# Conditioning sections and broadcasts of a decoder block moved between TensorE and the other engines

## The chip, the cores and the metric

The kernel runs on one core of a Trainium2 chip. The core has five engines with instruction streams of their own: TensorE (matmuls; PE in the profile), VectorE (DVE), ScalarE (ACT), GpSimd (POOL) and SyncE (SP), whose queue here starts nearly all loads from memory. Each engine executes its instructions in order and waits on semaphores for the others. The metric is the time of one execution on the device in microseconds (us); lower is better.

## What is computed

A decoder block for T = 256 tokens of D = 1024 channels, in float32. A conditioning vector `c` gives six rows that shift, scale and gate; then come a projection to 8192 columns, a convolution branch and a gated recurrence, and a mixture of 32 experts of which each token uses 4.

```python
mod = c_act @ w_ada[l] + b_ada[l]          # c_act = silu(c); six rows of 1024
sh1, sc1, ga1, sh2, sc2, ga2 = split(mod, 6)
h = rmsnorm(x, g_mix) * (1.0 + sc1) + sh1
p = h @ w_in[l]                             # 1024 x 8192
y_conv = conformer_conv(p[conv a], p[conv b], ...)   # 31 taps, layernorm, silu, projection
y_hg   = hgrn2(p[q], p[f], p[i], p[g], ...)          # recurrence, norm, gate, projection
merged = sigmoid(p[gc]) * y_conv + sigmoid(p[gh]) * y_hg
x  = x + ga1 * (merged @ w_out)
h2 = rmsnorm(x, g_ffn) * (1.0 + sc2) + sh2
x  = x + ga2 * moe(h2, w_router, b_router, w1, b1, w2, b2)   # top 4 of 32 experts, SwiGLU
out = rmsnorm(x, g_final)
```

## The kernel before

**Loads.** All weights come in tiles of 1 MB (128 partitions of 8 KB) into a ring of 22 slots (`big`, `NSLOT`). `load()` (L123) issues the next tile of a fixed order on SP's queue; the table `LOADS` says how many loads are issued each time a slot is given back by `free()`, and `fetch()` returns a tile. A load whose slot is still in use waits on SP's queue, and so do all behind it. At most eight loads are under way, since each takes one of eight semaphores.

**Start.** ScalarE squares x, TensorE adds the squares up (`ssp`), ScalarE copies the result (`sss`), TensorE gives the total to all partitions (`ss`), and ScalarE and VectorE make `rs` = 1/rms (L225). The first third of the conditioning (shift and scale 1) comes in eight tiles of `w_ada` ("ada0"), each through `mod_first` (TensorE, then a copy `mod0s` on ScalarE) and `h_tile`, which makes one eighth of `h`. This part stands in a block whose order on TensorE, ScalarE and VectorE is given by hand; behind it a scheduler of the framework puts each engine's instructions in order.

**Products.** The 32 blocks of `w_in`, n = 0 to 31 (128 x 8 x 256), are split in two halves each into a high and a low part (`split_half`): ScalarE casts (L371), GpSimd or VectorE subtracts (L373), by the tables `SPLIT_DVE` and `SPLIT_HALF`. "Unit n" is block n. `block_product` then runs 48 matmuls (L387). Blocks 0 to 3 are done during the start. What comes out of a block goes on: sigmoids (L695), 31 conv taps for each of 8 channel tiles (L438, VectorE, 240 steps), the recurrence (`hgrn_half`), and behind all taps a layer norm, whose sums TensorE makes (`mup`, `mu`) and which stands on TensorE ahead of block 25. Behind block 31 come the projections `ho`, `co` and `wo`, four units each, split like the blocks.

**Conditioning, later sections.** `mod_section(j)` makes one of four other rows: j = 1 gives `sh2`, 2 gives `g2`, 3 gives `ga2`, 0 gives `ga1`. Each has four chunks of `w_ada`, (j,0) to (j,3), 128 x 2 x 1024. One step is taken behind each block n in `MOD_AT`: 5, 7, 8, 11 for j = 1; 12 to 15 for j = 2; 18, 22, 25, 26 for j = 3; 27, 28, 30, 31 for j = 0. A chunk is 8 matmuls of 32 rows (L327), in which the column of `c_act` is the stationary operand; the results of the four column groups are copied (`mods`) and picked out by further matmuls (`mt`, `bb`) or, for `ga1`, by four broadcasts of GpSimd (L348, L349). `b_ada` is one loaded tile, added by matmuls for j = 0 and 3. In `hgrn_out` four more broadcasts of GpSimd (L605) give the norm `orr` to all partitions (`ors`).

**Experts.** For each expert, `first_layer` (L981) uses 8 tiles of w1, `turn` (L998, L1001) transposes the result, and `second_layer` (L1014) uses 4 tiles of w2. The rows of w1's tiles are 8 KB for each partition; w2's tile is read as "(k p) d -> p k d", two pieces of 4 KB for each partition.

Of the kernel before, what the change touches and what calls it, by code (L numbers as in the profile page):

```python
# [1402 lines left out]
```

## Time and profile before

| what | value |
|---|---|
| median of 3 runs | 1365.07 us (1362.7 to 1365.19) |
| profiled execution | 1363.14 us, its span 1361.4 us |
| granted TensorE clock, mean | 0.974 |
| busy: TensorE / VectorE / ScalarE / GpSimd | 1239.0 / 493.4 / 236.1 / 151.2 us |
| read from memory | 477.63 MB |
| products' first block behind the start (n=4) | from 59.96 us |
| first expert's products | from 399.34 us |

The profile is of one execution. The shares of busy time are means over stages that have different limits: the span has a first phase, up to the experts, in which all engines work and the transfers pause, and a second, in which TensorE and the transfers do nearly everything.

### The profile page before, as it was taken

To read this page: it belongs to the slowest core of one execution; us is meant where nothing else is said; L and a number is where in the kernel's file an instruction comes from. 1 tells how busy PE (TensorE), PEld (TensorE's weight loads), DVE (VectorE), ACT (ScalarE), POOL (GpSimd) and SP (SyncE) were. 2 spreads that over 40 slices of the span, in tenths; PEclk is the share of its full clock that TensorE was granted. 3 is DMA by queue.
4 is the path that set the end of the run, shared out by engine and by line. 5 is a ranking of instruction groups with operands and counts; after the bars stand their busy time and mean duration, and the time that the engine had idled before them with its cause. 6 is when DMAs were issued, how large, how long until landed. Compare 5 with 4: busy or idle time off the path is not lost. (4 is left out here: it accounts for less than half of the span.)

```text
span 1361.4 us, 18807 instructions
## 1 busy us (share of the span) xinstructions
PE 1239.0 (91%) x7749; PEld 667.7 (49%) x7749; DVE 493.4 (36%) x976; ACT 236.1 (17%) x387; POOL 151.2 (11%) x71
## 2 busy tenths in 40 slices
PE   6999999987899998999999999888888898898997
PEld 3998787687874343434334433232333433333432
DVE  4489999533843221122222312111221211222212
ACT  4445434742330000000000000000000000000012
POOL 2267435122300000000000000000000000000000
PEclk7999989998999998999999999999999998999999
DMA  9993336654679999999999999999999999999992
GB/s 380 411 371 131 120 125 229 247 217 151 236 299 404 417 414 416 407 415 415 415 414 416 416 417 416 415 416 415 416 415 414 412 416 416 391 389 415 415 409 80
DMA packets 87400, 481.07 MB, mean 353 GB/s; under 512 B 7488, under 2 KB 8768, under 8 KB 47808
## 3 DMA queue, kind: packets, MB, share of 16 engines
q1 hardware_dynamic: 86800, 477.99, 87.0%
q8 instruction: 121, 1.98, 0.6%
q10 hardware_dynamic: 432, 0.72, 0.1%
q14 instruction: 47, 0.39, 0.1%
HBM read 477.63 MB, written 1.05 MB: 352 GB/s over the span
## 5 line engine op out<-in xcount | busy, mean ns | idle before, releaser
L981 PE MATMUL u_gl<-w_w,xg 128*64 128x512 f32 x1024 | 286.9, 603 | 31.5 <-DMA w_w<-in_w_dram 19.1
L981 PE MATMUL u_lin<-w_w,xg 128*64 128x512 f32 x1024 | 285.2, 599 | 3.9 <-issue 3.9
L1014 PE MATMUL yp<-w_w,actT 128*64 128x512 f32 x992 | 219.7, 595 | 11.8 <-ACT actT L1001 11.8
L988 DVE TENSOR_SCALAR gl<-u_gl 128x512 f32<-128x512 f32 (+1 forms) x33 | 22.2, 675 | 424.1 <-PE u_gl L981 424.1
L981 PEld LDWEIGHTS u_gl<-w_w,xg 128*64 128x64 f32 x1024 | 82.2, 138 | 167.6 <-issue 100.4
L981 PEld LDWEIGHTS u_lin<-w_w,xg 128*64 128x64 f32 x1024 | 86.6, 138 | 149.8 <-issue 149.8
L989 ACT ACTIVATE si<-gl 128x512 f32<-128x512 f32 (+1 forms) x33 | 20.3, 617 | 745.3 <-DVE gl L988 745.3
L387 PEld LDWEIGHTS p_ps<-h,ws 128*128 128x128 f32 x1152 | 141.0, 193 | 12.8 <-issue 7.1
L387 PE MATMUL p_ps<-h,ws 128*128 128x256 f32 x1152 | 145.6, 286 | 0.0
L1014 PEld LDWEIGHTS yp<-w_w,actT 128*64 128x64 f32 x992 | 68.6, 137 | 144.6 <-issue 123.3
L1021 DVE TENSOR_TENSOR ys<-yp,ga 64x512 f32<-64x512 f32 x62 | 42.7, 689 | 260.0 <-PEq L1262 135.7
L373 POOL TENSOR_TENSOR ws<-w_in,ws 128x1024 fp32r<-128x1024 f32 x45 | 113.3, 2534 | 119.6 <-ACT ws L371 111.3
L438 DVE SCALAR_TENSOR_TENSOR cv<-u,pre,cv 128x255 f32<-128x255 f32 (+25 forms) x240 | 95.1, 457 | 8.7 <-ACT cv L435 7.8
L951 PE MATMUL xg_ps<-o,w_x 128*128 128x128 f32 (+1 forms) x544 | 67.1, 282 | 12.1 <-issue 7.6
L951 PEld LDWEIGHTS xg_ps<-o,w_x 128*128 128x128 f32 x544 | 64.0, 196 | 25.2 <-DVE gl L988 12.9
L371 ACT CAST ws<-w_in 128x1024 fp32r<-128x1024 f32 x64 | 65.9, 1046 | 43.4 <-PE p_ps L387 20.9
L1026 PE MATMUL acc<-ys,owt 128*128 128x512 f32 (+1 forms) x128 | 59.1, 603 | 2.2 <-PEq L1230 1.7
L955 DVE TENSOR_SCALAR xg<-xg_ps,g,sh 128x128 f32<-128x128 f32 (+1 forms) x136 | 45.4, 396 | 18.9 <-PE xg_ps L951 18.3
L1026 PEld LDWEIGHTS acc<-ys,owt 128*128 128x128 f32 (+1 forms) x128 | 22.9, 189 | 39.0 <-issue 25.1
L387 PE MATMUL ho_ps<-o,ws 128*128 128x256 f32 x192 | 24.9, 294 | 13.0 <-POOL ws L373 13.0
L387 PEld LDWEIGHTS ho_ps<-o,ws 128*128 128x128 f32 x192 | 24.5, 202 | 14.0 <-POOL ws L373 13.2
L387 PE MATMUL wo_ps<-ws,mg 128*128 128x256 f32 x192 | 26.0, 295 | 3.7 <-ACT ws L371 1.8
(269 smaller groups left out, 965.6 us busy)
## 6 DMA issues: line engine op xcount, KB each, us to landing
w_w<-in_w_dram SPq DMA_DIRECT2D x383, 1024.0 KB, 20.0
...
```

The lines of the kernel that those rows point to most:

```text
L371: nc.scalar.copy(out=to[:, 0], in_=w[:, ks, :])
L373: (nc.vector if dve else nc.gpsimd).tensor_tensor(out=to[:, 1], in0=w[:, ks, :], in1=to[:, 0].bitcast(F32), op=ALU.subtract)
L387: nc.tensor.matmul(out, lhsT=lt, rhs=rh, start=first and kt == 0 and i == 0, stop=kt == KT - 1 and i == 2, skip_group_check=not first)
L438: nc.vector.scalar_tensor_tensor(out=cv[:, ct, s:], in0=u[i][:, m, :T - s], scalar=tap, in1=cv[:, ct, s:], op0=ALU.mult, op1=ALU.add)
L951: nc.tensor.matmul(ps[:, i, cs], lhsT=x2[:, t, kt * P:(kt + 1) * P], rhs=o[:, 0, t, cs], start=t == 0, stop=t == NT - 1)
L955: nc.vector.tensor_scalar(out=xg[h][:, i, cs], in0=ps[:, i, cs], scalar1=g2[:, kt:kt + 1], scalar2=sh2[:, kt:kt + 1], op0=ALU.mult, op1=AL ...
L981: nc.tensor.matmul(up[nb][g * 64:(g + 1) * 64, :], lhsT=xg[kt // 4][:, kt % 4, i * CAP:(i + 1) * CAP], rhs=w[:, c:c + 512], start=False, s ...
L988: nc.vector.tensor_scalar(out=gl[:, c], in0=up[0][:, c], scalar1=LIMIT, scalar2=None, op0=ALU.min)
L989: nc.scalar.activation(si[:, c], gl[:, c], AF.Sigmoid, scale=ALPHA)
L1014: nc.tensor.matmul(yp[g * 64:(g + 1) * 64, :], lhsT=aT[:, kt % 4, kt // 4, :], rhs=w[:, kk, g * 512:(g + 1) * 512], start=False, stop=kt = ...
L1021: nc.vector.tensor_tensor(out=ys[g][i * CAP:(i + 1) * CAP, :], in0=yp[gs, :], in1=ga2[gs, :], op=ALU.mult)
L1026: nc.tensor.matmul(acc[t][g], lhsT=owt[rows, t * P:(t + 1) * P], rhs=ys[g][rows, :], start=False, stop=False)
```

## The change

Four edits. (1) In `mod_section` the matmuls of the chunks are gone. Each half chunk (128 x 1024) is multiplied by its column of `c_act` and added to `acc`, which lies in the slot of the section's first chunk. For j = 1 and 2 ScalarE multiplies (L327, L329 of the changed kernel) and GpSimd adds (L330); for j = 3 and 0 VectorE does both in one step (L332), but for the first half, which ScalarE multiplies. At the end matmuls with ones add `acc` up over the partitions. The rows of `b_ada` for `ga1` and `ga2` come by broadcasting loads; the tile `bada` is gone, and `LOADS` begins with 18 instead of 19 and differs in later entries. (2) The broadcasts of GpSimd become matmuls into PSUM. (3) w2's tiles are read as "(p k) d", one piece of 8 KB for each partition. (4) `turn` takes columns with a stride of 2 to match that.

```diff
...
     prm = of_pre(PR_COLS)
-    bada = of_pre(512)[:32, :]
...
-        if n == MOD_AT[0]:
-            queue(("bada",), None, bada_d, bada)
...
-                queue(("w2", e, k2), [P, 2, D], w2_d[e, k2 * 2 * P:(k2 + 1) * 2 * P, :].rearrange("(k p) d -> p k d", p=P))
+                queue(("w2", e, k2), [P, 2, D], w2_d[e, k2 * 2 * P:(k2 + 1) * 2 * P, :].rearrange("(p k) d -> p k d", k=2))
...
         nonlocal ga1
-        m = bank(f"mod{j}")
+        if j == 0:
+            ga1 = [temp("ga1") for _ in range(2)]
+            for b in range(2):
+                nc.sync.dma_start(out=ga1[b], in_=bada_d[4 + b, :].partition_broadcast(P))
+        elif j == 3:
+            for b in range(2):
+                nc.sync.dma_start(out=ga2[b * 64:(b + 1) * 64, :], in_=bada_d[10 + b, :].partition_broadcast(64))
         for k2 in range(4):
             w = fetch(("ada", j, k2))
...
             for h in range(2):
-                for b in range(2):
-                    g = 2 * h + b
-                    nc.tensor.matmul(m[g * 32:(g + 1) * 32, :], lhsT=cact[2 * k2 + h],
-                                     rhs=w[:, h, b * 512:(b + 1) * 512], start=k2 == 0 and (h == 1 or j in (1, 2)), stop=k2 == 3)
-            free()
+                cs = csig[:, 2 * k2 + h:2 * k2 + h + 1]
+                if k2 + h == 0:
+                    acc = w[:, 0, :]
+                    nc.scalar.activation(acc, acc, AF.Copy, scale=cs)
+                elif j in (1, 2):
+                    nc.scalar.activation(w[:, h, :], w[:, h, :], AF.Copy, scale=cs)
+                    nc.gpsimd.tensor_tensor(out=acc, in0=w[:, h, :], in1=acc, op=ALU.add)
+                else:
+                    nc.vector.scalar_tensor_tensor(out=acc, in0=w[:, h, :], scalar=cs, in1=acc, op0=ALU.mult, op1=ALU.add)
+            if k2 > 0:
+                free()
             yield
-        sb = temp(f"mods{j}")
-        nc.scalar.copy(out=sb, in_=m)
         if j in (1, 2):
             mt = bank("mt")
             for kt in range(KT):
-                nc.tensor.matmul(mt[:, kt:kt + 1], lhsT=sb[:, (kt % 4) * P:(kt % 4 + 1) * P], rhs=selb[kt // 4],
-                                 start=True, stop=True)
+                nc.tensor.matmul(mt[:, kt:kt + 1], lhsT=acc[:, kt * P:(kt + 1) * P], rhs=ones[:, 0:1], start=True, stop=True)
...
         elif j == 0:
...
-                nc.gpsimd.partition_broadcast(ga1[b], sb[b * 32:b * 32 + 1, :])
-                nc.gpsimd.partition_broadcast(other, sb[b * 32 + 64:b * 32 + 65, :])
-                nc.vector.tensor_tensor(out=ga1[b], in0=ga1[b], in1=other, op=ALU.add)
+                gb = bank("gb")
+                nc.tensor.matmul(gb, lhsT=ones, rhs=acc[:, b * 512:(b + 1) * 512], start=True, stop=True)
+                nc.vector.tensor_tensor(out=ga1[b], in0=gb, in1=ga1[b], op=ALU.add)
         else:
             bb = bank("bb")
...
-            nc.scalar.copy(out=ga2, in_=bb)
+            nc.vector.tensor_tensor(out=ga2, in0=bb, in1=ga2, op=ALU.add)
+        free()
...
-            ob = temp("ors")
-            nc.gpsimd.partition_broadcast(ob, orr[32 * hp:32 * hp + 1, :])
+            ob = bank("ors")
+            nc.tensor.matmul(ob, lhsT=ident[:, 32 * hp:32 * hp + 1].to_broadcast([P, P]), rhs=orr, start=True, stop=True)
...
+    def pick_columns(src, j):
+        return src[:, j // 2 * 2 * P + j % 2:(j // 2 + 1) * 2 * P:2]
...
+            c = pick_columns(li, j) if pieces == 1 else li[:, j * P:(j + 1) * P]
+            nc.tensor.transpose(ta[:, j * P:(j + 1) * P], c, ident)
...
```

The scheduler decides where the new instructions stand. On ScalarE, in the start, these rows stood behind the sigmoid of `c` (`pre`) before (`sss`, `rs` and `mod0s` as above):

```order
L234 ACTIVATE pre<-pre 128x8
L246 COPY sss<-ssp 128x256
L225 ACT_TABLE_LOAD
L225 ACTIVATE rs<-ss,eps 128x256
L268 ACT_TABLE_LOAD
L268 ACTIVATE pre<-pre 128x16
L289 COPY mod0s<-mod_156 128x256
```

And in the changed kernel, where `w_ada_1_0` is chunk (1,0) and `w_ada_1_1` chunk (1,1):

```order
L231 ACTIVATE pre_72<-pre_72 128x8
L327 ACTIVATE w_ada_1_0_106<-w_ada_1_0_106,pre_72 128x1024
L329 ACTIVATE w_ada_1_0_106<-w_ada_1_0_106,pre_72 128x1024
L243 COPY sss_134<-ssp_125 128x256
L329 ACTIVATE w_ada_1_1_112<-w_ada_1_1_112,pre_72 128x1024 x2
L222 ACT_TABLE_LOAD
L222 ACTIVATE rs_138<-ss_136,eps_117 128x256
L265 ACT_TABLE_LOAD
L265 ACTIVATE pre_72<-pre_72 128x16
L286 COPY mod0s_164<-mod0_155 128x256
```

Two of the four multiplications stand ahead of `sss`, and all four ahead of the table load for `rs` and of every `mod0s`.

On GpSimd, behind the start, there were only splits (`w_in_104` is unit 5, then units 7, 8, 9 and the next; unit 6 is VectorE's):

```order
L373 TENSOR_TENSOR ws<-w_in_90,ws 128x1024 x2
L373 TENSOR_TENSOR ws<-w_in_104,ws 128x1024 x2
L373 TENSOR_TENSOR ws<-w_in_111,ws 128x1024 x2
L373 TENSOR_TENSOR ws<-w_in_218,ws 128x1024 x2
L373 TENSOR_TENSOR ws<-w_in_472,ws 128x1024 x2
```

In the changed kernel the adds of sections 1 and 2 stand between them (`w_ada_0_106` is `acc` of section 1, `w_ada_0_547` that of section 2; the other name is the chunk):

```order
L374 TENSOR_TENSOR ws<-w_in_90,ws 128x1024 x2
L330 TENSOR_TENSOR w_ada_0_106<-w_ada_2_288,w_ada_0_106 128x1024 x2
L330 TENSOR_TENSOR w_ada_0_106<-w_ada_3_543,w_ada_0_106 128x1024 x2
L330 TENSOR_TENSOR w_ada_0_547<-w_ada_0_547 128x1024
L374 TENSOR_TENSOR ws<-w_in_104,ws 128x1024 x2
L330 TENSOR_TENSOR w_ada_0_547<-w_ada_1_551,w_ada_0_547 128x1024 x2
L374 TENSOR_TENSOR ws<-w_in_110,ws 128x1024 x2
L330 TENSOR_TENSOR w_ada_0_547<-w_ada_2_601,w_ada_0_547 128x1024
L374 TENSOR_TENSOR ws<-w_in_217,ws 128x1024 x2
L330 TENSOR_TENSOR w_ada_0_547<-w_ada_2_601,w_ada_0_547 128x1024
L330 TENSOR_TENSOR w_ada_0_547<-w_ada_3_733,w_ada_0_547 128x1024 x2
L374 TENSOR_TENSOR ws<-w_in_471,ws 128x1024 x2
```

From the first add to the second split of unit 9 these are 19 operations, 11 adds and 8 splits.

On VectorE, the last conv taps stood together before, ahead of a step of the recurrence's output (`sg`) and of the layer norm's subtraction (L543):

```order
L438 SCALAR_TENSOR_TENSOR cv<-u,pre,cv 128x229
L438 SCALAR_TENSOR_TENSOR cv<-u,pre,cv 128x228
L438 SCALAR_TENSOR_TENSOR cv<-u,pre,cv 128x227
L438 SCALAR_TENSOR_TENSOR cv<-u,pre,cv 128x226
L593 SCALAR_TENSOR_TENSOR sg<-ob,pre,sg 128x512
L543 TENSOR_TENSOR cv<-cv,mus 128x2048
```

In the changed kernel the same place reads (`w_ada_0_2423` is `acc` of section 0):

```order
L439 SCALAR_TENSOR_TENSOR cv<-u,pre,cv 128x229
L332 SCALAR_TENSOR_TENSOR w_ada_0_2423<-w_ada_3_2844,pre,w_ada_0_2423 128x1024
L439 SCALAR_TENSOR_TENSOR cv<-u,pre,cv 128x228
L374 TENSOR_TENSOR ws<-w_in_2474,ws 128x1024
L439 SCALAR_TENSOR_TENSOR cv<-u,pre,cv 128x227
L332 SCALAR_TENSOR_TENSOR w_ada_0_2423<-w_ada_3_2844,pre,w_ada_0_2423 128x1024
L439 SCALAR_TENSOR_TENSOR cv<-u,pre,cv 128x226
L374 TENSOR_TENSOR ws<-w_in_2474,ws 128x1024
L594 SCALAR_TENSOR_TENSOR sg<-ob,pre,sg 128x512
L544 TENSOR_TENSOR cv<-cv,mus 128x2048
```

All 14 steps of sections 3 and 0 stand ahead of the last tap there, and two splits more than before.

## Rows read from the trace of the kernel before

**Rows 1.** Busy time by stretch, second phase: PE, PEld, DVE, ACT, POOL; clock, DMA share, GB/s.
```profile
400.00:425.00 25.00, 24.67 (x132) 10.95 (x130) 4.97 (x13) 1.59 (x3) 0.00 (x0) 1.00 0.92 365
425.00:800.00 375.00, 356.83 (x1728) 148.89 (x1724) 87.17 (x192) 18.42 (x33) 0.00 (x0) 0.99 1.01 414
```

**Rows 2.** List of waits, whole run: who waits for whom; us in total, times, longest.
```profile
SPq L123 <- DMA w_w<-in_w_dram: 387.1, 224, 3.2
```

**Rows 3.** Timeline of ScalarE, the start: start, duration, what, [idle before <- releaser].
```profile
12.20 1.28 ACT L225 ACT_TABLE_LOAD   x1
...
60.16 0.66 ACT L695 ACTIVATE sigb<-e_ps 128x256 f32<-128x256 f32 x2 [4.50 <-PE e_ps L387]
```

**Rows 4.** Timeline of TensorE: blocks n=4 and n=5, and the first mod chunk.
```profile
59.96 11.68 PE L387 MATMUL p_ps<-h,ws 128*128 128x256 f32 x96
71.57 1.06 PE L327 MATMUL mod<-w_ada,pre 128*32 128x512 f32 x8
```

**Rows 5.** Busy time by stretch, conv taps and HGRN (columns as in rows 1).
```profile
100.00:110.00 10.00, 10.00 (x118) 9.87 (x119) 8.02 (x21) 6.91 (x13) 6.89 (x3) 1.00 0.01 2
110.00:120.00 10.00, 10.00 (x182) 8.64 (x168) 8.30 (x15) 5.70 (x10) 9.86 (x5) 1.00 0.30 108
120.00:230.00 110.00, 102.85 (x1434) 88.50 (x1434) 108.89 (x202) 45.90 (x73) 53.92 (x22) 0.95 0.47 171
```

**Rows 6.** Timeline of TensorE ahead of n=25: the sums over the conv output.
```profile
230.31 0.40 PE L243 MATMUL mup<-cv,pre 128*32 128x256 f32 x1 [0.54 <-DVE cv L438]
```

**Rows 7.** Timeline of TensorE, the second stretch of ho's products.
```profile
315.83 15.55 PE L387 MATMUL ho_ps<-o,ws 128*128 128x256 f32 x116 [12.98 <-POOL ws L373]
```

**Rows 8.** Timeline of GpSimd in the same stretch.
```profile
313.44 4.67 POOL L373 TENSOR_TENSOR ws<-w_ho,ws 128x1024 fp32r<-128x1024 f32 x2 [7.21 <-issue]
```

**Rows 9.** Timeline of SP's queue: issue of chunks (1,0) and (1,1).
```profile
29.25 0.38 SPq L123 DMA_DIRECT2D w_ada<-in_wada_dram  x1
...
36.55 0.38 SPq L123 DMA_DIRECT2D w_ada<-in_wada_dram  x1
```

**Rows 10.** Loads of L123 issued in the first 60 us: time to landing.
```profile
DMA to landing us min/median/max: 9.0/17.4/21.5
```

**Rows 11.** Costliest groups of the page: busy us, mean ns of one, idle before.
```profile
L438 DVE SCALAR_TENSOR_TENSOR cv<-u,pre,cv 128x255 f32<-128x255 f32 (+25 forms) x240 | 95.1, 457 | 8.7 <-ACT cv L435 7.8
...
L371 ACT CAST ws<-w_in 128x1024 fp32r<-128x1024 f32 x64 | 65.9, 1046 | 43.4 <-PE p_ps L387 20.9
L1026 PE MATMUL acc<-ys,owt 128*128 128x512 f32 (+1 forms) x128 | 59.1, 603 | 2.2 <-PEq L1230 1.7
```

**Rows 12.** Groups of GpSimd by form, whole run (columns as in rows 11).
```profile
L373 POOL TENSOR_TENSOR ws<-w_in,ws 128x1024 fp32r<-128x1024 f32 x45 | 113.3, 2534 | 119.6 <-ACT ws L371 111.3 <-DVE cv L438 8.3
L373 POOL TENSOR_TENSOR ws<-w_ho,ws 128x1024 fp32r<-128x1024 f32 x5 | 12.1, 2420 | 27.9 <-ACT ws L371 20.7 <-issue 7.2
```

**Rows 13.** Groups of VectorE by form in 109 to 231 us.
```profile
L478 DVE TENSOR_TENSOR k<-k,f 128x512 f32<-128x512 f32 x12 | 14.1, 1174 | 0.0
...
L373 DVE TENSOR_TENSOR ws<-w_in,ws 128x1024 fp32r<-128x1024 f32 x4 | 4.8, 1212 | 0.0
```

**Rows 14.** Timeline of VectorE, two steps of one form in the start.
```profile
17.52 0.48 DVE L300 SCALAR_TENSOR_TENSOR xT<-xT,pre,rs 128x256 f32<-128x256 f32 x1
...
34.80 2.53 DVE L300 SCALAR_TENSOR_TENSOR xT<-xT,pre,rs 128x256 f32<-128x256 f32 x1
```

**Rows 15.** Timeline of GpSimd at the second of these steps.
```profile
34.66 4.88 POOL L373 TENSOR_TENSOR ws<-w_in,ws 128x1024 fp32r<-128x1024 f32 x2 [4.98 <-ACT ws L371]
```

**Rows 16.** Busy time by stretch between landings of expert tiles (columns as in rows 1).
```profile
463.65:473.89 10.24, 9.84 (x42) 3.69 (x40) 2.77 (x4) 1.22 (x2) 0.00 (x0) 1.00 1.03 416
473.89:493.77 19.88, 19.72 (x98) 6.95 (x95) 4.63 (x12) 0.63 (x1) 0.00 (x0) 1.00 1.01 417
493.77:503.92 10.15, 9.81 (x64) 5.63 (x65) 4.10 (x10) 0.96 (x2) 0.00 (x0) 1.00 1.02 402
507.20:524.60 17.40, 17.08 (x74) 6.70 (x70) 2.77 (x4) 1.06 (x2) 0.00 (x0) 1.00 1.01 418
```

More of the change, by code (lines that the diff above doesn't have):

```diff
@@ L41 @@
 MOD_EXTRA = {}
-LOADS = (19, 0, 0, 0, 0, 0, 1, 0, 0, 1, 0, 0, 0, 0, 1, 2, 2, 2, 2, 0, 0, 1, 0, 0, 1, 1, 0, 0, 1, 0, 0, 1, 1, 0, 0, 1, 0, 0, 0, 0, 0, 0, 0, 0, 0, 1, 0, 0, 0, 1, 1, 0, 0, 0, 0, 0, 0, 1, 1, 0, 0, 1, 1, 0, 0, 1, 0, 0, 0, 0, 0, 0, 1, 0, 0, 1, 1, 0, 0, 1, 0, 0, 0, 0, 0, 1, 0, 0, 1, 1, 0, 0, 1, 1, 2, 0, 0, 0, 0, 3, 1, 0, 0, 1, 1, 0, 0, 1, 1, 3, 0, 0, 0, 0, 0, 0, 0, 0, 0, 1, 1, 1, 0, 1, 1, 2, 0, 0, 1, 0, 0, 1, 0, 0, 1, 0, 0, 1, 1, 0, 0, 0, 0, 0, 1, 1, 0, 0, 0, 0, 1, 1, 2, 1, 0, 0, 1, 0, 0, 1, 0)
+LOADS = (18, 0, 0, 0, 0, 0, 1, 0, 0, 1, 0, 0, 0, 0, 1, 2, 2, 2, 2, 0, 0, 1, 0, 0, 1, 0, 0, 1, 0, 0, 1, 1, 0, 0, 1, 0, 0, 0, 0, 0, 0, 0, 0, 0, 1, 0, 0, 0, 1, 1, 0, 0, 0, 1, 0, 0, 1, 1, 0, 0, 1, 0, 0, 0, 0, 0, 0, 1, 0, 0, 1, 1, 0, 0, 1, 0, 0, 0, 0, 0, 1, 0, 0, 1, 1, 0, 0, 1, 1, 2, 0, 0, 0, 0, 1, 1, 0, 0, 3, 1, 0, 0, 1, 1, 3, 0, 0, 0, 0, 0, 0, 0, 0, 0, 1, 1, 1, 0, 1, 1, 2, 1, 0, 0, 1, 0, 0, 1, 0, 0, 1, 0, 0, 1, 1, 0, 0, 0, 0, 0, 2, 1, 0, 0, 0, 0, 1, 1, 2, 1, 0, 0, 1, 0, 0, 1, 0, 0, 1, 1, 4)
 TAPS = (1, 0, 0, 0, 5, 4, 10, 6, 5, 5, 13, 6, 16, 14, 17, 11, 5, 8, 0, 6, 0, 0, 0, 0, 0, 3, 13, 9, 17, 15, 9, 5)
@@ L315, in mod_section @@
         nonlocal ga1
-        m = bank(f"mod{j}")
+        if j == 0:
[5 more added lines that the diff above has]
+                nc.sync.dma_start(out=ga2[b * 64:(b + 1) * 64, :], in_=bada_d[10 + b, :].partition_broadcast(64))
         for k2 in range(4):
             w = fetch(("ada", j, k2))
-            if k2 == 0 and j in (0, 3):
-                for b in range(2):
-                    nc.tensor.matmul(m[b * 32:(b + 1) * 32, :],
-                                     lhsT=ident[:32, 4 + 2 * j + b:5 + 2 * j + b].to_broadcast([32, 32]),
-                                     rhs=bada, start=True, stop=False)
-            for h in range(2):
-                for b in range(2):
-                    g = 2 * h + b
-                    nc.tensor.matmul(m[g * 32:(g + 1) * 32, :], lhsT=cact[2 * k2 + h],
-                                     rhs=w[:, h, b * 512:(b + 1) * 512], start=k2 == 0 and (h == 1 or j in (1, 2)), stop=k2 == 3)
-            free()
+            for h in range(2):
+                cs = csig[:, 2 * k2 + h:2 * k2 + h + 1]
[9 more added lines that the diff above has]
+                free()
             yield
-        sb = temp(f"mods{j}")
-        nc.scalar.copy(out=sb, in_=m)
         if j in (1, 2):
@@ L344, in mod_section @@
         elif j == 0:
-            ga1 = [temp("ga1") for _ in range(2)]
             for b in range(2):
-                other = temp("ga1b")
-                nc.gpsimd.partition_broadcast(ga1[b], sb[b * 32:b * 32 + 1, :])
-                nc.gpsimd.partition_broadcast(other, sb[b * 32 + 64:b * 32 + 65, :])
-                nc.vector.tensor_tensor(out=ga1[b], in0=ga1[b], in1=other, op=ALU.add)
+                gb = bank("gb")
+                nc.tensor.matmul(gb, lhsT=ones, rhs=acc[:, b * 512:(b + 1) * 512], start=True, stop=True)
+                nc.vector.tensor_tensor(out=ga1[b], in0=gb, in1=ga1[b], op=ALU.add)
         else:
@@ L353, in mod_section @@
             for b in range(2):
-                nc.tensor.matmul(bb[b * 64:(b + 1) * 64, :], lhsT=selb[b].to_broadcast([P, 64]), rhs=sb,
+                nc.tensor.matmul(bb[b * 64:(b + 1) * 64, :], lhsT=ones[:, 0:64], rhs=acc[:, b * 512:(b + 1) * 512],
                                  start=True, stop=True)
-            nc.scalar.copy(out=ga2, in_=bb)
+            nc.vector.tensor_tensor(out=ga2, in0=bb, in1=ga2, op=ALU.add)
+        free()
     parts = {}
@@ L738, in block_kernel @@
         step(norms, 1)
-        if n == MOD_AT[0]:
-            fetch(("bada",))
         if n in MOD_AT:
@@ L1065, in small_first @@
         for j in range(4):
-            nc.tensor.transpose(ps[:, j * P:(j + 1) * P], a[:, j * P:(j + 1) * P], ident)
+            nc.tensor.transpose(ps[:, j * P:(j + 1) * P], pick_columns(a, j), ident)
         gl, li = (ps.rearrange("p (j h c) -> p j h c", j=4, h=2)[:, :, h, :] for h in range(2))
@@ L1160, in w2s @@
                                 nc.gpsimd.dma_start(out=w, in_=w2_d[bass.ds(e, 1), k2 * 2 * P:(k2 + 1) * 2 * P, :].rearrange(
-                                    "o (k p) d -> p (o k) d", p=P))
+                                    "o (p k) d -> p (o k) d", k=2))
                                 return w
```

1 line of the change is left out of this document (removed).

## The prediction

> **What bounds the kernel now.** I read the stretches first. From 425 us on the transfers are busy all the time (share 1.01, against 0.92 just before) [rows 1]. In the list of waits SP's queue waits 387.1 us, in 224 pieces, for its own earlier expert tiles [rows 2]. So the experts last as long as their transfers. That stream starts when the first expert hands back slots of the ring, which is full by then: what delays the first expert delays the end one for one.
>
> Phase 1 is a chain, read from the timelines. ScalarE loads the table for `rs` at 12.20, right behind its copy `sss` of the sums of squares [rows 3], and n=4 of the products starts at 59.96 [rows 4]. VectorE is busy 8.02 and 8.30 of 10 us in 100–120 and 108.89 of the 110 us after that [rows 5], and TensorE waits for the last tap before `mup` at 230.31, ahead of n=25 [rows 6]: there VectorE sets the time. In `ho` TensorE ends an idle time of 12.98 us, at 315.83, on a split of GpSimd, which itself started only after 7.21 us without work [rows 7, 8].
>
> The profiled execution took 1363.14 us, 1.7 outside its span and 1.9 under the median of the runs; I sum against 1363.1.
>
> **The start (+44).** ScalarE works in order, and in the new order four scales of the chunks (1,0) and (1,1) stand ahead of the copy `sss` and of the table load for `rs`. Their loads were issued at 29.25 and 36.55 [rows 9]; the median time to landing in the first 60 us is 17.4 [rows 10], so an estimate for the landings is 46.7 and 54.0. The queue ahead of them is the same but for 64 KB. Behind `sss` waits TensorE (`ss`, then the whole `mod_first` chain), behind the table load every `mod0s` copy. Two scales at about 1.05 us, as the cast of the same shape [rows 11], put the table load at 54.0 + 2.1 = 56.1 instead of 12.20: +44. With the shortest and the longest landing (9.0, 21.5) it is 35.5 and 48. Loads that have landed meanwhile may give back a little; the lower end takes that in. I keep 44, and n=4 starts at 104.
>
> **n=5 to 10 (+9).** GpSimd's new order holds 19 operations from the adds of (1,2) to the second split of unit 9, where before there were 8 splits. An add of 128x1024 is priced as the split of that shape, 2.42 to 2.53 us [rows 12]. The first two adds fit before n=4. The scales of (1,3) and (2,0) stand behind the last `sigb`, which ended 0.9 after n=4's start [rows 3, 4], so the next add starts at 104 + 0.9 + 1.05 = 106. Four operations of 2.45 give the first half of unit 5 at 115.8, where n=5 wants it at 110 (two blocks take 11.68 [rows 4]): +6. Twelve more give the first half of unit 9 at 145.2; n=9, four blocks of 5.84 after 115.8, wants it at 139.2: +6. Three chunks of `mod` at 1.06 [rows 4] are gone: −3. Sum +9; with the adds hidden beside TensorE it is −3, with every operation at 2.53 about +10. I take +9: nothing else of GpSimd's work could give way to the new operations.
>
> **n=11 to 25 (+17).** Before the last tap VectorE now does the 14 scale-and-add steps of sections 3 and 0, and two more splits. Nothing of that form is in the trace; nearest is its split of the same 128x1024, 1212 ns [rows 13]: 16 × 1.21 = 19.4. Four more taps stand ahead of the last wait, 4 × 0.46 = 1.8 [rows 11]. Less the 3.7 us that VectorE has free in 100–120 [rows 5] that is +17. TensorE saves seven chunks here, 7 × 1.06 = 7.4, and gains nothing from them as long as VectorE is late. If VectorE is not what is late, the term is −7; if each step takes 2.53, the longest that a two-input step of VectorE took beside a split of GpSimd [rows 14, 15], it is 17 + 14 × 1.3 = +35. I take 1.21, VectorE's mean for that shape beside GpSimd's splits in this very stretch. Late next are `mup`, `mu` and n=25.
>
> **n=26 to the experts (−16).** Six chunks less on TensorE, −6.4; six matmuls of 128x512 come in for the broadcasts, 6 × 0.6 [rows 11] = +3.6; so −3. GpSimd's four broadcasts of `ga1`, and the 7.21 us with no work that follow them before its next split [rows 8], no longer stand between TensorE and the second unit of `ho`: −13, the whole idle time [rows 7]. If another split is late instead, only the 7.2 go: bounds −13 and −7. The four broadcasts of `ors` stand far ahead of `ho`, whose wait was another one; that edit counts as matmuls alone.
>
> **Hidden edits (0).** The two pairs of row broadcasts by DMA, the slot held by `acc` and the new LOADS table fall where the transfers are far from full, 0.30 in 110–120 and 0.47 in 120–230 [rows 5]; if that cover were gone, the broadcasts, which write 0.79 MB, would cost less than a tile, 2.5 us. The transposes with stride 2 are as many as before.
>
> **w2 rows (−6).** Stretches cut at landings: while the four w2 tiles of an expert land, 416 and 402 GB/s (mean 409); while w1 tiles land, whose rows are 8 KB already, 417 and 418 [rows 16]. A tile is 1.049 MB: 2.564 against 2.511 us, 0.053 × 124 tiles = −6.5, taken as −6. Bounds from 416 and 402 alone: −1 and −12. The Trainium skill, "DMA: Bandwidth & Descriptors", section "Why small descriptors are slow", gives a fixed cost of about 3 cycles to each packet; on 128 beats against 256 this is 1.2% of a tile, by an estimate from that page −3.7 in all; the trace shows 2.1%.
>
> Sum: 44 + 9 + 17 − 16 − 6 = +48, so 1363.1 + 48 = **1411 us**. Its own range is 1397 to 1425 (start −8/+4, GpSimd ±4, VectorE's overlap with other waits ±6, tail +6, w2 −6/+4, roughly half of them at once).
>
> **Rivals.**
> - *VectorE has room*: its new steps fall into waits that the later GpSimd work makes, and n=11 to 25 saves TensorE's 7 us. For it: 3.7 us free in 100–120, and 11 us of waiting on TensorE at n=5 and 9. Against: the last 100 us before `mup` are full [rows 5, 6]. 1411 − 17 − 7 = 1387.
> - *VectorE and GpSimd block each other*: `L300` took 0.48 us with GpSimd idle and 2.53 while it split [rows 14, 15]. The 128x512 products of 109–231 took 1174 ns, near the 1212 of a split twice as large [rows 13], so some are held up there already. With all 14 steps doubled, 1411 + 18 = 1429. The Trainium skill, "SBUF — State Buffer", section "Who interferes with whom", states the rule that speaks against this change: a VectorE step with two SBUF inputs and a GpSimd operation that reads SBUF lock each other out for a whole instruction; the trace's 2.53 agrees.
> - *The ring makes it good* (the other side): the experts' loads go out at the times of before although the products are late, so the end stays where the transfers put it, and w2's 6 us are a gain: 1363 − 6 = 1357. It decides if the loads need no slot that a late product holds, that is, if the first expert's delay costs under 6 us at the end. For it: transfers bound the second phase. Against: the transfers stood at 0.92 and less until the first expert freed slots [rows 1].
> - *The scales do not hold ScalarE* (the change does not do there what its order says, or the two chunks land by 12 us): 1411 − 44 = 1367. Against: sixteen tiles of 2.5 us stand ahead of them on one queue.
>
> **How the numbers follow.** A measurement of this kernel can tell about 0.2% (2.7 us) from no change. Chances: my forecast 0.58, VectorE has room 0.20, blocking 0.13, the ring 0.04, no hold 0.05. The predicted time is the forecast's. For 8 in 10 the range reaches into both neighbours, which end 24 below and 18 above it: 1381 to 1432; outside lie the ring, no hold and the far ends. Slower: 0.58 + 0.20 + 0.13 and half of no hold, 0.93; the same 0.03 (the other half); faster 0.04.
>
> **What would show it.** Right: ScalarE idle from about 13 to 47 before a scale, released by the load of `w_ada`; the table load near 56; n=4 near 104; GpSimd nearly without a gap from 106 to 148 and waits of TensorE of 5 to 6 us on it at n=5 and n=9; a TensorE wait of over 10 us on VectorE before n=25; no 13 us stall in `ho`; the first expert near 453 instead of 399; w2 stretches at 417 GB/s. Wrong: scales that start before 30 us, VectorE with free time in the 100 us before the last tap, or transfers that reach 1.01 well before the first expert.

## The result, and the profile after

The changed kernel takes 1430.4 us (median of 4 runs, 1428.85 to 1431.41) against 1363.88 us before: ratio 1.0489, 95% interval 1.0468 to 1.051, 66.5 us slower. The forecast was 1411 us in a range of 1381 to 1432; the result lies 1.6 us inside the upper end. Its profiled execution took 1428.85 us, span 1427.2, so the two profiles are 65.8 us apart.

ScalarE's timeline in the start (start, duration, what, [idle before <- releaser]), the answer to [rows 3]:

```profile
45.15 1.15 ACT L327 ACTIVATE w_ada<-w_ada,pre 128x1024 f32<-128x1024 f32 x1 [34.00 <-DMA w_ada<-in_wada_dram]
46.20 1.13 ACT L329 ACTIVATE w_ada<-w_ada,pre 128x1024 f32<-128x1024 f32 x1
47.24 0.35 ACT L243 COPY sss<-ssp 128x256 f32<-128x256 f32 x1
52.98 2.19 ACT L329 ACTIVATE w_ada<-w_ada,pre 128x1024 f32<-128x1024 f32 x2 [5.39 <-DMA w_ada<-in_wada_dram]
55.19 1.28 ACT L222 ACT_TABLE_LOAD   x1
```

ScalarE stands idle for 34 us on the load of chunk (1,0) and for 5.4 more on that of (1,1); the table load comes at 55.19 instead of 12.20. TensorE's timeline, the answer to [rows 4, 6 and 7]:

```profile
47.65 1.22 PE L249 MATMUL ss<-sss,con 128*128 128x256 f32 x2 [36.03 <-ACT sss L243]
...
104.02 6.50 PE L388 MATMUL p_ps<-h,ws 128*128 128x256 f32 x50
115.56 24.66 PE L388 MATMUL p_ps<-h,ws 128*128 128x256 f32 x192 [5.04 <-POOL ws L374]
...
146.15 18.72 PE L388 MATMUL p_ps<-h,ws 128*128 128x256 f32 x142 [5.93 <-POOL ws L374]
...
309.32 1.06 PE L240 MATMUL mup<-cv,pre 128*32 128x256 f32 x2 [21.16 <-DVE cv L439]
...
311.50 6.90 PE L388 MATMUL p_ps<-h,ws 128*128 128x256 f32 x48
...
369.21 23.59 PE L388 MATMUL ho_ps<-o,ws 128*128 128x256 f32 x192
392.63 1.86 PE L626 MATMUL rb<-wr,sh 128*128 128x32 f32 x16
...
468.02 1.03 PE L980 MATMUL u_gl<-w_w,xg 128*64 128x512 f32 x4
```

The same places in the kernel before (n=9 to n=11, n=25, the start of `ho`, and `rb` behind it):

```profile
92.20 17.54 PE L387 MATMUL p_ps<-h,ws 128*128 128x256 f32 x144
...
232.07 6.10 PE L387 MATMUL p_ps<-h,ws 128*128 128x256 f32 x48
...
293.47 9.38 PE L387 MATMUL ho_ps<-o,ws 128*128 128x256 f32 x76
...
331.22 1.86 PE L625 MATMUL rb<-wr,sh 128*128 128x32 f32 x16
```

n=4 starts at 104.02 (before 59.96). TensorE waits for GpSimd's split at n=5 (5.04) and at n=9 (5.93), and 21.16 us for VectorE's last tap ahead of n=25; `ho` has no wait left. The stretches and groups of VectorE behind n=10, the answer to [rows 5 and 13] (busy time by stretch; then groups by form in 159 to 310 us, with mean ns):

```profile
125.00:175.00 50.00, 42.04 (x446) 41.09 (x446) 40.90 (x96) 30.01 (x44) 45.11 (x20) 0.93 0.37 137
175.00:300.00 125.00, 98.07 (x1392) 92.36 (x1392) 125.00 (x216) 47.86 (x75) 59.45 (x24) 0.89 0.39 141
```

```profile
L478 DVE TENSOR_TENSOR q<-q,f 128x512 f32<-128x512 f32 x12 | 19.0, 1585 | 0.0
L332 DVE SCALAR_TENSOR_TENSOR w_ada<-w_ada,pre,w_ada 128x1024 f32<-128x1024 f32 x12 | 18.4, 1530 | 0.0
L479 DVE TENSOR_TENSOR k<-k,f 128x512 f32<-128x512 f32 x12 | 16.9, 1405 | 0.0
...
L332 DVE SCALAR_TENSOR_TENSOR w_ada<-w_ada,pre 128x1024 f32<-128x1024 f32 x2 | 2.5, 1272 | 0.0
```

VectorE is full from 175 to 300. Its free time lies in 125 to 175, where of the eight chunks of sections 3 and 0 only the first has been asked for (at 153.44). In the expert phase the transfers move 418 GB/s where they moved 414 [rows 1]; the stretch:

```profile
500.00:875.00 375.00, 358.56 (x1728) 145.74 (x1726) 86.51 (x186) 19.63 (x35) 0.00 (x0) 1.00 1.01 418
```

Term by term, from the two profiles:

| stretch | forecast | measured | from |
|---|---|---|---|
| start, to n=4 | +44 | +44.1 | 104.02 − 59.96 |
| n=4 to the end of n=11 | +9 | +11.1 | 164.87 − 109.74, less the above |
| to n=25 | +17 | +24.3 | 311.50 − 232.07, less the above |
| to the first expert | −16 | −10.8 | 468.02 − 399.34 = 68.7, less the above |
| experts | −6 | −2.9 | 65.8 − 68.7 |

### The profile page after: what moved, and what is told of

Read it like the earlier page. It is cut to its first block, busy times and chain, and to the rows that moved or that the text cites. A ratio compares the mean times of both kernels' runs of the same rounds, so it can differ in the third digit from the quotient of the medians.

```text
span 1427.2 us, 18586 instructions
## 1 busy us (share of the span) xinstructions
PE 1234.9 (87%) x7625; PEld 676.1 (47%) x7625; DVE 514.5 (36%) x991; ACT 252.0 (18%) x400; POOL 177.3 (12%) x77
## 5 line engine op out<-in xcount | busy, mean ns | idle before, releaser
L388 PE MATMUL p_ps<-h,ws 128*128 128x256 f32 x1152 | 149.9, 292 | 11.0 <-POOL ws L374 11.0
L388 PEld LDWEIGHTS p_ps<-h,ws 128*128 128x128 f32 x1152 | 144.9, 198 | 15.7 <-POOL ws L374 11.4
L439 DVE SCALAR_TENSOR_TENSOR cv<-u,pre,cv 128x243 f32<-128x243 f32 (+27 forms) x240 | 94.4, 454 | 15.8 <-ACT cv L436 15.8
L372 ACT CAST ws<-w_in 128x1024 fp32r<-128x1024 f32 x64 | 64.7, 1047 | 65.9 <-POOL ws L374 23.4
L950 PE MATMUL xg_ps<-o,w_x 128*128 128x128 f32 (+1 forms) x544 | 66.5, 281 | 7.7 <-issue 5.1
L330 POOL TENSOR_TENSOR w_ada<-w_ada,w_ada 128x1024 f32<-128x1024 f32 x12 | 29.7, 2471 | 22.8 <-ACT w_ada L329 22.3
```

Source lines behind the costliest of these rows:

```text
L330: nc.gpsimd.tensor_tensor(out=acc, in0=w[:, h, :], in1=acc, op=ALU.add)
L372: nc.scalar.copy(out=to[:, 0], in_=w[:, ks, :])
L388: nc.tensor.matmul(out, lhsT=lt, rhs=rh, start=first and kt == 0 and i == 0, stop=kt == KT - 1 and i == 2, skip_group_check=not first)
L439: nc.vector.scalar_tensor_tensor(out=cv[:, ct, s:], in0=u[i][:, m, :T - s], scalar=tap, in1=cv[:, ct, s:], op0=ALU.mult, op1=ALU.add)
L950: nc.tensor.matmul(ps[:, i, cs], lhsT=x2[:, t, kt * P:(kt + 1) * P], rhs=o[:, 0, t, cs], start=t == 0, stop=t == NT - 1)
```

## Experiments

All ratios are to the kernel before in the same session. The theory that they test: three waits (at the start, on GpSimd ahead of units 5 and 9, on VectorE ahead of n=25) go to the end one for one, and w2's rows and the broadcasts give a little back.

**w2_rows**: w2's rows and the transposes alone.

```diff
-                queue(("w2", e, k2), [P, 2, D], w2_d[e, k2 * 2 * P:(k2 + 1) * 2 * P, :].rearrange("(k p) d -> p k d", p=P))
+                queue(("w2", e, k2), [P, 2, D], w2_d[e, k2 * 2 * P:(k2 + 1) * 2 * P, :].rearrange("(p k) d -> p k d", k=2))
```

> The kernel before with the 8 KB rows of w2 alone (and the transposes with stride 2 that belong to them). By the prediction's term a w2 tile takes 2.51 us where it took 2.56, and 124 tiles give -6 us: ratio 0.9955. If the row length does nothing, the ratio is 1.000. If the expert phase gains only part of it because TensorE, not the transfers, limits its first 400 us, the ratio is 0.997 to 0.999; then the landings come 2.49 us apart but the expert phase is shorter by less than 124 x 0.065 us.

Measured 1355.46 us against 1364.58, ratio 0.9945 (0.9928 to 0.9961): −7.5 us, but its six runs go from 1346.56 to 1359.59. The median time between the landings of two w2 tiles in the middle of the expert phase was 2.550 us before and 2.486 with the long rows, the same as w1's; the six kernels with the old rows have 2.547 to 2.556, the seven with the new ones 2.484 to 2.487. The difference times 124 is 7.9 us. The expert phase (from the first expert to the end of the profile) is noisier: 955.0 to 966.7 us with the old rows, mean 961.5, and 947.4 to 961.0 with the new ones, mean 955.7. The term stands, a little larger than forecast in the tile. The estimate from the Trainium skill, "DMA: Bandwidth & Descriptors", section "Why small descriptors are slow" (1.2% of a tile, −3.7, from the cost of a packet alone), is too small: the tile shows 2.5%.

**te_bcast**: the broadcasts alone, the sections left on TensorE.

```diff
-            nc.gpsimd.partition_broadcast(ob, orr[32 * hp:32 * hp + 1, :])
+            nc.tensor.matmul(ob, lhsT=ident[:, 32 * hp:32 * hp + 1].to_broadcast([P, P]), rhs=orr, start=True, stop=True)
...
-                nc.gpsimd.partition_broadcast(ga1[b], sb[b * 32:b * 32 + 1, :])
-                nc.gpsimd.partition_broadcast(other, sb[b * 32 + 64:b * 32 + 65, :])
-                nc.vector.tensor_tensor(out=ga1[b], in0=ga1[b], in1=other, op=ALU.add)
+                gb = bank("gb")
+                nc.tensor.matmul(gb, lhsT=selb[b].to_broadcast([P, P]), rhs=sb, start=True, stop=True)
+                nc.scalar.copy(out=ga1[b], in_=gb)
```

> The kernel before with the broadcasts of ors and ga1 on TensorE alone. By the prediction the idle time of 12.98 us in ho goes and six matmuls come in: about -10 us, ratio 0.993, and TensorE's wait in ho is under 2 us. If another split is late next, only the 7.2 us behind the broadcasts go: -4 us, ratio 0.997. If later stages take the gain back, as 7 us were taken back behind ho in the changed kernel, the first expert starts 3 to 5 us earlier and the ratio is 0.997 too, but without a wait in ho.

Ratio 0.9954 (0.9937 to 0.997), −6.3 us. TensorE's timeline:

```profile
298.79 23.59 PE L386 MATMUL ho_ps<-o,ws 128*128 128x256 f32 x192
322.22 1.86 PE L624 MATMUL rb<-wr,sh 128*128 128x32 f32 x16
```

`ho` runs 23.4 us without a wait where it took 37.7, −14.3; from n=25 to `ho` the new matmuls cost +4.1; the first expert starts 9.0 earlier. The expert phase of this profile is 4.1 us longer than before, which lies within the spread of that phase; that it gives something back is not shown.

**both**: the two edits together, with no other change.

> The kernel before with both: w2's rows and TensorE's broadcasts, the conditioning sections left on TensorE. If the two terms add up: -16 us, ratio 0.988. If one of them is hidden: -6 to -10 us, 0.993 to 0.996. This version should beat both kernels.

1351.34 us, ratio 0.9883 (0.9858 to 0.9909). That is −16.0 us, and the two alone sum to −13.8; within the intervals they add up, and this version is faster than both kernels.

**no_hold**: the changed kernel, in which the scales cannot come ahead of `h`.

```diff
+    late = fix.tile([P, KT], F32, name="late")
+    nc.vector.scalar_tensor_tensor(out=late, in0=s1, scalar=0.0, in1=csig, op0=ALU.mult, op1=ALU.add)
     mods = [mod_section(j) for j in SECTIONS]
...
-                cs = csig[:, 2 * k2 + h:2 * k2 + h + 1]
+                cs = late[:, 2 * k2 + h:2 * k2 + h + 1]
```

> The changed kernel, with the columns of c_act for the sections read from a copy that is made from the last column of h's scale, so that no scale can stand ahead of the start's sums. By the prediction the start's 44 us go: n=4 starts at 60. The adds of section 1 that GpSimd did in the start's wait then come between the sigmoids and unit 5, five operations more, so n=5 waits some 13 us instead of 6: -44 + 7, ratio to before 1.022 (1394 us). If the delay of the start is passed on only in part, because other engines make it good, the gain is under 30 us and the ratio is over 1.027. If GpSimd's adds fit beside the start, the ratio is 1.016.

1394.95 us, ratio 1.0221 (1.0204 to 1.0239). TensorE's timeline:

```profile
59.86 5.92 PE L388 MATMUL p_ps<-h,ws 128*128 128x256 f32 x48
80.26 0.80 PE L388 MATMUL p_ps<-h,ws 128*128 128x256 f32 x2 [14.48 <-ACT ws L372]
84.07 16.20 PE L388 MATMUL p_ps<-h,ws 128*128 128x256 f32 x121 [3.01 <-POOL ws L374]
```

The start's 44 us are gone, and TensorE waits 14.48 and 3.01 us at n=5 instead. The ratio is the expected one, but not for the expected reason: the longer wait ends on ScalarE, not on GpSimd's adds. ScalarE's timeline ahead of the cast of unit 5 (L372):

```profile
72.06 2.19 ACT L329 ACTIVATE w_ada<-w_ada,late 128x1024 f32<-128x1024 f32 x2 [7.35 <-DMA w_ada<-in_wada_dram]
77.08 1.15 ACT L327 ACTIVATE w_ada<-w_ada,late 128x1024 f32<-128x1024 f32 x1 [2.84 <-DMA w_ada<-in_wada_dram]
...
79.18 1.98 ACT L372 CAST ws<-w_in 128x1024 fp32r<-128x1024 f32 x2
```

Scales of later chunks stand ahead of the cast and wait for their loads, 7.35 and 2.84 us: the mechanism of the start again, one place further on. Only the 3.01 us behind it end on GpSimd. Before the last taps TensorE waits as in the changed kernel:

```profile
275.88 1.06 PE L240 MATMUL mup<-cv,pre 128*32 128x256 f32 x2 [21.60 <-DVE cv L439]
```

**hold**: the kernel before with the wait alone, nothing else.

```diff
+    nc.scalar.copy(out=held[:, 0:1], in_=loaded[("ada", 1, 0)][:, 0, 0:1])
...
     rs = temp("rs")
+    nc.scalar.copy(out=held[:, 1:2], in_=loaded[("ada", 1, 1)][:, 0, 0:1])
     rsqrt_mean(rs[:, :T], ss, D)
```

> The kernel before, with the wait of the start alone: ScalarE copies one column of chunk (1,0) ahead of the copy sss and one column of chunk (1,1) ahead of the table load for rs, and nothing else changes. If the wait is the whole of the first term and goes to the end one for one: n=4 at 103 to 104, ratio 1.032 (+44 us). If the ring or slack later in phase 1 makes part of it good, n=4 starts at 104 all the same but the first expert starts less than 35 us late and the ratio is under 1.025.

1406.66 us against 1367.13, ratio 1.0312 (1.0279 to 1.0345). ScalarE:

```profile
45.50 0.19 ACT L238 COPY held<-w_ada 128x1 f32<-128x1 f32 x1 [34.31 <-DMA w_ada<-in_wada_dram]
...
53.04 0.19 ACT L261 COPY held<-w_ada 128x1 f32<-128x1 f32 x1 [7.08 <-DMA w_ada<-in_wada_dram]
53.25 1.28 ACT L225 ACT_TABLE_LOAD   x1
```

n=4 is 42.3 us late, the first expert 41.8, the profile's end 42.6; by the interval of the ratio it is 38 to 47 us. Two copies of one column cost that: the wait is the term, and nothing behind it makes it good. The rival of the ring falls.

**sec30**: before, with sections 3 and 0 alone in the new form (and the new LOADS table, without which the ring overflows).

```diff
+    def mod_section(j):
+        return (mod_section_off if j in (3, 0) else mod_section_pe)(j)
```

> The kernel before, with sections 3 and 0 alone in the new form (VectorE's scale-and-add, rows of b_ada by broadcasting loads, ga1 by TensorE; the new LOADS table, no bada tile); sections 1 and 2 stay on TensorE. If VectorE has no free time between n=11 and n=25, n=25 is 21 to 25 us late (14 steps and 2 to 3 splits), TensorE saves about 5 us behind it and the wait in ho goes (-13): about +6, ratio 1.003 to 1.008. If VectorE had room, n=25 is not late and the ratio is 0.987. If GpSimd and VectorE block each other in the steps, over half of the 14 steps take over 2 us and the ratio is 1.015.

Ratio 1.0091 (1.0065 to 1.0116), above the 1.003 to 1.008 expected and below the rival's 1.015. n=25 starts 31 us late, not 21 to 25; TensorE waits 25.81 us for the taps, and the steps are dearer than in the changed kernel (groups by form, 104 to 261 us):

```profile
L375 DVE SCALAR_TENSOR_TENSOR w_ada<-w_ada,pre,w_ada 128x1024 f32<-128x1024 f32 x12 | 20.6, 1721 | 0.5 <-DMA w_ada<-in_wada_dram 0.5
...
L375 DVE SCALAR_TENSOR_TENSOR w_ada<-w_ada,pre 128x1024 f32<-128x1024 f32 x2 | 6.4, 3204 | 0.0
```

That is 27.0 us for the 14 steps, 1.93 each: nine took 1.26 to 1.29 us, and five, which met an operation of GpSimd, 2.98 to 3.43.

**sec12**: the same with sections 1 and 2 alone.

```diff
+        return (mod_section_off if j in (1, 2) else mod_section_pe)(j)
```

> The kernel before, with sections 1 and 2 alone in the new form (ScalarE scales, GpSimd adds; the new LOADS table); sections 3 and 0 and all broadcasts as before. In its order the scales of chunk (1,0), not of (1,1), stand ahead of sss: the start is 35 us late. GpSimd then has 17 operations more than before up to unit 9's split, or two more than in the changed kernel: another +10 to +15 by n=11. Behind it VectorE has no new step; if its term was the 14 steps alone, the delay at n=25 is that at n=11, the ratio 1.033 to 1.037; if GpSimd's adds slow VectorE's products too, n=25 is 5 us later than that, 1.04.

Ratio 1.0327 (1.0293 to 1.036). n=4 starts at 95.3, 35.4 late, as expected from one chunk instead of two; at n=5 TensorE waits 5.42 us for GpSimd's split and at n=10 3.38, and the end of n=11 is 45.5 late. n=25 is 49.0 late. The 3.5 between these two are no sign that the adds slow VectorE: loads_only, without the adds, has 3.4 in the same stretch.

**late30**: no_hold, with sections 3 and 0 behind the last tap, and loads put off where the ring has no room.

```diff
-MOD_AT = (5, 7, 8, 11, 12, 13, 14, 15, 18, 22, 25, 26, 27, 28, 30, 31)
+MOD_AT = (5, 7, 8, 11, 12, 13, 14, 15, 24, 25, 26, 27, 28, 29, 30, 31)
...
         elif j == 3:
+            nc.vector.scalar_tensor_tensor(out=late2, in0=cv[:, :, T - 1], scalar=0.0, in1=csig, op0=ALU.mult, op1=ALU.add)
...
-                cs = late[:, 2 * k2 + h:2 * k2 + h + 1]
+                cs = (late if j in (1, 2) else late2)[:, 2 * k2 + h:2 * k2 + h + 1]
```

> The variant without the hold of the start, in which the steps of sections 3 and 0 also wait: their chunks come behind n=24 to n=31 and their columns of c_act are read from a copy made behind the last conv tap (the loads that the table grants are put off where the ring has no room). If VectorE was the limit up to the last tap, n=25 comes 20 to 24 us earlier than without this (at 254 to 258 instead of 278), and as VectorE has some 25 of 61 us free behind it, the ratio falls from 1.022 to 1.005 to 1.010. If the held slots delay the loads of the last blocks, n=25 comes earlier all the same but ho does not, and the ratio stays above 1.015.

Ratio 1.0102 (1.0077 to 1.0127), by the ratios 16 us less than no_hold. n=25 starts at 262.95, 15 earlier; the other 5 to 9 us did not come, as TensorE still waits 9.59 for the last tap, and VectorE, among its last taps, 3.69 for TensorE's `mt` of section 2. The 14 steps ahead of the taps are the larger part of VectorE's term, not all of it.

**loads_only**: before, with the changed kernel's LOADS table in place of its own.

```diff
-LOADS = (19, 0, 0, 0, 0, 0, 1,
...
+LOADS = (18, 0, 0, 0, 0, 0, 1,
...
```

> The kernel before with the changed kernel's LOADS table and nothing else. In every variant with that table the stretch from rb to the first expert took 73 to 75.5 us, in every variant with the old one 67.6 to 68.1. If the table is the reason (it hands slots to w_co and w_wo in another order, and the second unit of wo is then cast behind the router's squares), the stretch takes 74 to 75 us here too and the ratio is 1.004 to 1.006. If the sections' new form is the reason, the stretch takes 68 us and the ratio is 1.000.

Ratio 1.0052 (1.0031 to 1.0073). From `rb` to the first expert it takes 74.9 us where before has 67.7: the table alone does it. The difference arises in `wo`, and ScalarE's timeline shows how; the casts of `wo` before, and then here:

```profile
357.78 3.88 ACT L371 CAST ws<-w_wo 128x1024 fp32r<-128x1024 f32 x4
```

```profile
362.22 1.99 ACT L371 CAST ws<-w_wo 128x1024 fp32r<-128x1024 f32 x2
...
374.02 0.42 ACT L814 ACTIVATE tq<-w_x 128x256 f32<-128x256 f32 x1 [0.24 <-DVE w_x L813]
...
374.44 1.98 ACT L371 CAST ws<-w_wo 128x1024 fp32r<-128x1024 f32 x2
```

With the old table ScalarE casts the first two units of `wo` one behind the other; with the new one the second stands behind the router's squares (`tq`), which need `wo`'s first products, and TensorE starts that unit at 375.52, as its first cast ends. The table does one thing more: n=25 starts 3.9 us late, though no work was added. `q` and `k`, two products of the recurrence on VectorE, take 1774 and 1412 ns there, before 1159 and 1174; other products of the recurrence get shorter.

**spread**: the changed kernel with all four sections elsewhere: 1 and 2 behind n=10, 3 and 0 behind the taps, and loads put off where the ring has no room.

```diff
+MOD_AT = (10, 11, 12, 13, 14, 15, 18, 20, 24, 25, 26, 27, 28, 29, 30, 31)
...
+        if j == 1:
+            nc.vector.scalar_tensor_tensor(out=late, in0=f[:, 1, 0:KT], scalar=0.0, in1=csig, op0=ALU.mult, op1=ALU.add)
```

> The changed kernel with all four sections moved, not undone: sections 1 and 2 behind n=10 to 20, with columns that are read from a copy made from the first f block (n=10), sections 3 and 0 behind the last tap. If the loss lay in three places (start, GpSimd ahead of unit 5, VectorE ahead of the taps), all three go: n=4 at 60, n=11 at 104 to 106, no wait on GpSimd at n=5 and n=9; VectorE's products beside GpSimd's adds make n=25 some 5 to 10 us late, and wo's 7 us stay: ratio 0.993 to 1.003. If GpSimd's 35 us of adds cost as much in any place, the ratio is over 1.01.

Ratio 1.008 (1.0048 to 1.0111), a miss. The first two places are cured: n=4 at 59.6, n=11 at 99.9, 4 earlier than before. But n=25 starts at 259.6, 27.5 late, though VectorE has no step of the sections ahead of it (groups by form, 100 to 258 us; the last row is the taps, all forms together):

```profile
L485 DVE TENSOR_TENSOR k<-k,f 128x512 f32<-128x512 f32 x12 | 23.5, 1956 | 0.0
L484 DVE TENSOR_TENSOR q<-q,f 128x512 f32<-128x512 f32 x12 | 19.6, 1631 | 0.0
```

```profile
L445 DVE SCALAR_TENSOR_TENSOR cv<-u,pre,cv 128x246 f32<-128x246 f32 (+28 forms) x167 | 66.7, 457 | 0.6
```

Beside GpSimd's adds the recurrence's products `k` and `q` take 1956 and 1631 ns, before 1174 [rows 13] and 1159: 9.4 + 5.7 = 15 us more for these 24. Busy time of each engine from n=11 to n=25 (PE, PEld, DVE, ACT, POOL), here and in the kernel before:

```profile
100.00:259.60 159.60, 124.07 (x1622) 115.97 (x1620) 148.99 (x236) 75.01 (x110) 108.77 (x43) 0.83 0.36 133
```

```profile
103.84:232.07 128.23, 120.76 (x1693) 103.87 (x1691) 123.80 (x233) 57.66 (x94) 67.27 (x28) 0.96 0.43 157
```

Of the 31.4 us that this stretch is longer, 25.2 are VectorE's busy time, with 3 instructions more; the others of its two-input products and its splits got longer too. The taps, half of VectorE's work there, take 457 ns as before.

That GpSimd is the reason shows in single instructions. One `k` beside two adds of GpSimd, and one while GpSimd has no work (VectorE's lines, then GpSimd's):

```profile
149.39 2.88 DVE L485 TENSOR_TENSOR k<-k,f 128x512 f32<-128x512 f32 x1
198.98 0.69 DVE L485 TENSOR_TENSOR k<-k,f 128x512 f32<-128x512 f32 x1
```

```profile
146.53 5.19 POOL L336 TENSOR_TENSOR w_ada<-w_ada,w_ada 128x1024 f32<-128x1024 f32 x2
212.74 5.21 POOL L380 TENSOR_TENSOR ws<-w_in,ws 128x1024 fp32r<-128x1024 f32 x2 [19.20 <-ACT ws L378]
```

In all the kernels a `q` or `k` that meets no operation of GpSimd takes 0.67 to 0.69 us, and one that meets one up to 2.94. As a sum: take for each form of VectorE's instructions, the taps aside, the shortest time that it has in any kernel, and add up what the instructions from n=11 to n=25 took beyond it. That held time is 26 us in the kernel before and 51 in spread, of which 0.3 us or less lie in instructions beside which GpSimd did nothing. The products have both inputs in SBUF; of the taps' two tensors one, `u`, lies in PSUM. That is the rule of the Trainium skill, "SBUF — State Buffer", section "Who interferes with whom": a VectorE step with two SBUF inputs and a GpSimd operation that reads SBUF exclude each other. The trace agrees, 0.69 against 2.88 us for `k`. So GpSimd's work (41.5 us of busy time more) is not free beside the recurrence: VectorE pays some 25 of them. How much it pays in a given order depends on which instructions meet: in loads_only the held time is 31 us with no work added, so some 5 of the 25 may belong to the table, which spread has too.

**off30**: "both", with sections 3 and 0 on VectorE behind the last tap and the old table (first entry 18, loads put off where the ring is full).

```diff
+MOD_AT = (5, 7, 8, 11, 12, 13, 14, 15, 24, 25, 26, 27, 28, 29, 30, 31)
...
+                cs = late2[:, 2 * k2 + h:2 * k2 + h + 1]
...
+        return (mod_section_off if j in (3, 0) else mod_section_pe)(j)
```

> The version with w2's rows and TensorE's broadcasts, and in addition sections 3 and 0 on VectorE, but only behind the last conv tap (chunks behind n=24 to 31, columns from a copy that is made behind the taps), with the old LOADS table but for the first entry; sections 1 and 2 stay on TensorE. If what the two sections cost was their place ahead of the taps, n=25 is where it was (231 to 234) and TensorE's six chunks less give 6 to 8 us: ratio 0.982 to 0.984, faster than all others. If the 20 us of steps make the layer norm or ho late instead, the ratio is 0.988 or more, and TensorE waits on VectorE between n=26 and ho.

1342.98 us, ratio 0.984 (0.9813 to 0.9868), the lowest of all, 22 us under before; the interval overlaps that of "both", which was taken in another session. The ratio is the expected one, but not for the reason expected: n=25 starts at 242.0, not at 231 to 234, `ho` at 299.7 and the first expert at 390.7, where "both" has 231.4, 298.4 and 389.5. The difference to "both" lies behind that, in an expert phase of 948.7 us against 961.0, which does the same work; w2_rows had 947.4 in its profile, and "both" itself had two of six runs under 1344. So the sections gave nothing here, and what makes some expert phases 10 us shorter is open.

## Why the prediction was right, and where its steps were off

The places and the direction were right, the sum was not: it gave +48, and the two profiles are 65.8 us apart. The result lies outside the range that the forecast had for itself (1397 to 1425), and in the stated one only because that reached up to the rival of blocking (1429), which was at work in one of the four places where the sum fell short. That it lies in the range is luck in part.

**The start: right.** 44.1 us, shown by no_hold (gone) and hold (there alone, 42.3). The landings, estimated at 46.7 and 54.0 from the median, came at about 45 and 53.

**One for one: right.** hold loses 42.3 at n=4 and 42.6 at the end of its profile.

**n=5 to 10: right in the waits, 2 us short.** Waits of 5.04 and 5.93 on GpSimd were forecast as 6 and 6; sec12 has such waits too, and in spread, where the adds stand elsewhere, n=11 starts 4 us earlier than before. What the sum left out is TensorE's clock. Behind the two waits the granted clock has a mean of 0.94 and 0.91 of 2.4 GHz, as part of each stretch ran at 1.2 GHz, and was 1.00 in the same blocks before, which no wait of this kind interrupted (busy time by stretch, the clock third from the end; here, then before):

```profile
115.56:140.22 24.66, 24.66 (x192) 24.46 (x192) 15.80 (x33) 11.97 (x16) 24.50 (x10) 0.94 0.47 173
146.15:164.87 18.72, 18.72 (x148) 18.59 (x152) 16.72 (x46) 10.29 (x16) 15.14 (x7) 0.91 0.17 57
```

```profile
72.56:109.74 37.18, 37.18 (x316) 35.10 (x315) 32.58 (x87) 18.72 (x26) 25.79 (x11) 1.00 0.71 291
```

192 of the products' matmuls took 24.66 us, at the pace of n=4 and n=5 before (11.68 for 96 [rows 4]) 23.36; the next 142 took 18.72, before 17.54 for 144. Together that is 2.7 us more.

**n=11 to 25: mis-sized**, +24.3 instead of +17; this is the largest error. VectorE's busy time from the end of n=11 to n=25 grew from 117.9 to 142.9 us, by 25.0:

```profile
164.87:311.50 146.63, 107.88 (x1574) 100.60 (x1573) 142.87 (x236) 57.55 (x89) 68.43 (x28) 0.87 0.41 147
```

The 14 steps took 20.9 us (18.4 + 2.5) instead of 17: twelve took 1.27, two beside a split of GpSimd 2.70 and 2.98. Two more splits stand ahead of the last tap, as forecast, and a third between it and n=25 (7 × 1.21 in the stretch, before 4); one tap more lies in it, not four. `q` and `k` took 1585 and 1405 ns, 5.1 + 2.8 = 7.9 us more for the 24; the recurrence's other products took some 4 less. These durations come to some 28 us; as one step's record begins shortly before the last one's ends, 25.0 of them are busy time. The 3.7 us of free time were subtracted wrongly: VectorE has 3.8 left here of 4.4, and the room in 125 to 175 lies ahead of the chunks' loads. The rival "VectorE has room" falls with the full 125 us.

The rival of mutual blocking (chance 0.13), priced for all 14 steps, was at work in part. The held time (as under spread) is 33 us in the changed kernel, before 26: 3.2 more at the steps and 3.3 at the recurrence, near the 7.3 us by which the term was short. In sec30 the steps alone have 9. Whether the recurrence's part comes from the new work or from the new LOADS table is not shown: loads_only loses 3.4 us in this stretch by the table alone.

**Behind n=25: mis-sized**, −10.8 instead of −16. n=25 to `ho` gave −3.7 (forecast −3) and `ho` −14.3 (−13); +7.3 came back between `rb` and the first expert. The step that failed is "Hidden edits (0)": it asked of the new LOADS table only whether the transfers are full, and not what order of casts it leads to. loads_only shows 7.2 us there from the table alone.

**w2's rows: right in the tile** (2.550 to 2.486 us, forecast 2.564 to 2.511), and −7.5 us by runs alone; the −2.9 of the two profiles has the run-to-run changes of the expert phase in it.

The errors all go the same way: +2.1 at n=5 to 10, +7.3 at VectorE, +5.2 behind it and +3.1 at the experts, with 0.1 at the start the 17.8 us between 48 and 65.8. Adding up separate stretches found the places, because each ended on a wait that could be named. It missed what the same operations cost each other; the last 3.1 us lie within the spread of the expert phase.
